# ScalarE's drains moved one row group sooner, into the hold

## The chip, the cores and the metric

One core of one Trainium2 chip. The metric is device time in microseconds (us); a run's "span" is what the profile covers of it, from the first to the last instruction, some 1.3 us less.

## The reference

```python
# x: 16 x 2048 x 256, W: 256 x 256, rank 16, all float32
x_flat = x.reshape(-1, in_dim)
y = x_flat @ W
lora_out = x_flat @ lora_A
lora_out = lora_out * lora_E
lora_out = lora_out @ lora_B
y = y + scale * lora_out
# ... reshaped to batch x seq x out_dim
```

So 33.55 MB go in, 33.55 MB come out, and one 256 x 256 matrix (W plus the low-rank part, folded into it at the start) multiplies it all.

## The kernel before

The rows are cut into 4 chunks of 8.39 MB. Three "homes" in SBUF, the memory on the chip, hold a chunk each; results overwrite their inputs there. A chunk is worked through in 16 row groups, 64 in all, numbered from 0: GpSimd casts a group to bf16, TensorE transposes it, VectorE copies the transposition out of PSUM (the memory that TensorE writes to), TensorE multiplies, ScalarE copies the product from PSUM back into the home. SyncE issues the loads ("L") and stores ("S") in this order, all on one queue; behind the letter stand the chunk, its first row and the row after its last, of 64 in each partition ("A" loads `lora_A`):

```python
ORDER = [
    ("A",),
    ("L", 0, 0, 16),
    ("L", 0, 16, 40),
    ("L", 0, 40, 64),
    ("L", 1, 0, 32),
    ("L", 1, 32, 64),
    ("L", 2, 0, 64),
    ("S", 0, 0, 40),
    ("S", 0, 40, 64),
    ("L", 3, 0, 32),
    ("L", 3, 32, 64),
    ("S", 1, 0, 64),
    ("S", 2, 2, 62),
    ("S", 3, 0, 64),
]

SHARED = 2
END_ROWS = 2
SHARES = (slice(108, 113), slice(0, 108), slice(113, P))

HELD = (2, 0)
HOLDERS = (("S", 0, 0, 40),)

WARM_UP = 2

VECTOR_DRAINS = 12
GPSIMD_DRAINS = 10
SCALAR_DRAINS = 22

CG = 4
GPC = ROWS // CG
N_GROUPS = N_CHUNKS * GPC
```

SyncE's part. A load into a home waits for the stores of the chunk that was there; a store waits for a count that ScalarE raises:

```python
# ... (inside the loop over ORDER)
            kind, c, s, e = op
            at_home = home(c)[:, s:e, :]
            if kind == "L":
                for st in stored:
                    if st[1] == c - N_HOMES and st[2] < e and s < st[3]:
                        sync.wait_ge(stored[st], 16)
                ins = sync.dma_start(out=at_home, in_=x_chunks[c, :, s:e, :]).then_inc(loaded[op], 16)
                if n == 1:
                    opening.append(ins.ins.name)
            else:
                sync.wait_ge(s_done, ends.index((c * ROWS + e - 1) // CG) + 1)
                sync.dma_start(out=y_chunks[c, :, s:e, :], in_=at_home).then_inc(stored.get(op, stored_rest), 16)
        sync.wait_ge(shared_stored, 16 * len(SHARES))
```

VectorE, GpSimd and ScalarE each have a row of drains, which wait for chunk 2's load and then are executed, without working on any data:

```python
    def drain(engine, n):
        for op, landed in loaded.items():
            if op[1:3] == HELD:
                engine.wait_ge(landed, 16)
        for _ in range(n):
            engine.drain()
```

GpSimd is what makes the hold: chunk 2's first group (number 32) waits until chunk 0's first store has landed. At the end it issues small stores of the first two and last two of chunk 2's 64 rows in each partition ("the small stores" below), on a queue of its own.

```python
        for g in range(N_GROUPS):
            c, b = g // GPC, g % GPC * CG
            for op, landed in loaded.items():
                if op[1:3] == (c, b):
                    gpsimd.wait_ge(landed, 16)
            if (c, b) == HELD:
                drain(gpsimd, GPSIMD_DRAINS)
                for op in HOLDERS:
                    gpsimd.wait_ge(stored[op], 16)
            if g >= NS:
                gpsimd.wait_ge(s_turned, g - NS + 1)
            gpsimd.tensor_copy(out=stage[g % NS][:], in_=home(c)[:, b:b + CG, :]).then_inc(s_stage[g % UNROLL], 1)

        gpsimd.wait_ge(s_turned, N_GROUPS - NS + 1)
        gpsimd.drain().then_inc(s_stage[N_GROUPS % UNROLL], 1)
        gpsimd.wait_ge(s_shared, 1)
        for p in SHARES:
            share(gpsimd, p, shared_stored)
```

ScalarE, before:

```python
        for g in range(N_GROUPS):
            c, b = g // GPC, g % GPC * CG
            if (c, b) == HELD:
                drain(scalar, SCALAR_DRAINS)
            scalar.wait_ge(s_y, g + 1)
            scalar.copy(out=home(c)[:, b:b + CG, :], in_=psum_y[g % NY][:]).then_inc(s_free[(g + NY) % UNROLL], 1)
            if (c, b + CG) == (SHARED, ROWS):
                scalar.drain().then_inc(s_shared, 1)
            if g in ends:
                scalar.drain().then_inc(s_done, 1)
```

TensorE runs one group ahead, so that `turn(32)` stands in front of `multiply(31)`; that is why ScalarE's copy of group 31, the last of chunk 1, waits for the hold to end:

```python
        def turn(i, result=None):
            words = stage[i % NS][:].bitcast(FP32)
            staged = s_stage[i % UNROLL]
            for b in range(CG):
                if b == 0:
                    tensor.wait_ge(staged, 1)
                if b == CG - 1 and result is not None:
                    tensor.wait_ge(s_free[result % UNROLL], 1)
                ins = tensor.transpose(psum_xt[i % NT][:, b, :], words[:, b, :], ident[:])
                if b == 0:
                    ins.then_inc(staged, -1)
            ins.then_inc(s_turned, 1)
        # ...
        with tensor.Fori(0, N_GROUPS // UNROLL):
            for i in range(UNROLL):
                turn(i + 1, i)
                multiply(i)
```

## Time and profile before

| | before |
|---|---|
| time, median of the first 3 runs | 161.29 us (161.27 to 161.30) |
| chunk 2 landed; hold ended | 62.70; 75.04 us |
| copy of group 31; copy of group 32 starts | 79.11; 81.45 us |
| chunk 2's, chunk 3's store issued | 101.94; 122.82 us |
| chunk 1's, 2's, 3's store landed | 121.61; 139.97; 159.99 us |

Every time here is counted from the span's start. The page gives the shares over the span. The table by stretch gives them stage by stage. The chain of waits follows the last instruction back through what released it. The list of SyncE's waits says how long SyncE stood at each of its instructions. The prediction shows the lines.

```profile
SPq L300 <- SPq L300: 3.2, 1, 3.2
```

Line 300 is SyncE's very last wait, for the large stores. It began 3.2 us before it was met: everything else, the wait for the small stores and the closing steps of all engines, was over 3.2 us before the end.

### The profile page before, as it was taken

Reading aid. Unit: us, or ns where it says so; the run is one execution under the profiler, and the core shown is the slowest. Engines: PE = TensorE matmul, PEld = TensorE weight load, DVE = VectorE, ACT = ScalarE, POOL = GpSimd, SP = SyncE. Lnnn points to the kernel's source line nnn. Section 1 sums busy time; section 2 is a strip of 40 time slices with the busy share of each in tenths; the row PEclk is TensorE's granted clock in tenths of the full one; section 3 lists DMA queues with packets and bytes.
Section 4 is the critical chain, followed back from the end, with each engine's and each line's share of the span. In section 5 each row is a group of like instructions: output and inputs, shape, how many; then the busy total and the mean of one; then the engine's idle time right before and its main releaser. Section 6 shows DMA issues by size and latency. Waiting matters only on the chain.

```text
span 160.0 us, 2070 instructions
## 1 busy us (share of the span) xinstructions
PE 96.5 (60%) x782; PEld 84.4 (53%) x782; DVE 45.4 (28%) x66; ACT 66.0 (41%) x65; POOL 69.3 (43%) x73
## 2 busy tenths in 40 slices
PE   2769999999999900000999999999994000000000
PEld 1246899999999900000789999999993000000000
DVE  0113355555555500000155555555550000000000
ACT  3001477777777720000257777777775000000000
POOL 1072577777787400002577777778762000000000
PEclk9999999999999995555599999999999555555555
DMA  7999999999969997999999999989979997989986
GB/s 269 427 448 436 412 440 467 451 393 418 631 262 524 475 311 328 403 420 434 412 465 428 401 475 426 532 377 410 524 308 446 480 485 305 544 342 481 441 360 262
DMA packets 2451, 67.43 MB, mean 421 GB/s; under 512 B 512, under 2 KB 528, under 8 KB 784
## 3 DMA queue, kind: packets, MB, share of 16 engines
q1 hardware_dynamic: 2016, 66.60, 97.4%
q0 software_dynamic: 224, 0.52, 0.9%
q10 hardware_dynamic: 208, 0.28, 0.6%
q14 instruction: 3, 0.02, 0.0%
HBM read 33.85 MB, written 33.55 MB: 421 GB/s over the span
## 4 chain that ended last, share of the span: by engine, by line
PE 38%; DMA 33%; ACT 3%; POOL 1%; issue 1%; ACTq 0%; SPq 0%
DMA out_dram<-home 28%; PE psum_y L269 24%; PE psum_xt L258 13%; DMA home<-in_x_dram 5%; ACT home L221 3%; POOL stage L200 1%; PE psum_y L291 1%; SPq L147 0%; ACTq L175 0%; ACTq L225 0%
## 5 line engine op out<-in xcount | busy, mean ns | idle before, releaser
L200 POOL CAST stage<-home 128x1024 bf16<-128x1024 f32 x64 | 66.6, 1042 | 48.6 <-PE psum_xt L258 22.1
L221 ACT COPY home<-psum_y 128x1024 f32<-128x1024 f32 x64 | 64.7, 1012 | 54.8 <-PE psum_y L269 54.8
L269 PE MATMUL psum_y<-weff,xt 128*128 128x256 bf16 x512 | 69.1, 280 | 0.0
L242 DVE COPY xt<-psum_xt 128x1024 bf16<-128x1024 bf16 x64 | 44.3, 692 | 66.2 <-PE psum_xt L258 66.2
L258 PE MATMUL psum_xt<-ident,stage 128*128 128x128 f32 x260 | 42.2, 286 | 22.3 <-POOL stage L200 22.3
L269 PEld LDWEIGHTS psum_y<-weff,xt 128*128 128x128 bf16 x512 | 51.5, 101 | 6.2
L258 PEld LDWEIGHTS psum_xt<-ident,stage 128*128 128x128 f32 x260 | 32.4, 148 | 25.2 <-issue 23.6
L282 PE MATMUL psum_y<-ident 128*128 128x512 f32 x4 | 3.8, 1101 | 2.9 <-POOL ident L180 2.9
L282 PEld LDWEIGHTS psum_y<-ident 128*128 128x128 f32 x4 | 1.2, 325 | 3.9 <-POOL ident L180 2.9
L230 DVE TENSOR_SCALAR ate<-psum_y,e_sb 16x256 f32<-16x256 f32 x1 | 0.5, 471 | 7.2 <-DMA e_sb<-in_lora_E_dram 7.2
L168 POOL DMA_DIRECT2D out_dram<-home x3 | 2.0, 676 | 1.0 <-PE psum_xt L258 1.0
L221 ACT ACT_TABLE_LOAD x1 | 1.3, 1283 | 2.1 <-SPq L304 2.1
L291 PE MATMUL psum_y<-b_sb,ate 16*128 16x256 f32 x4 | 2.1, 670 | 0.0
L291 PEld LDWEIGHTS psum_y<-b_sb,ate 16*128 16x128 f32 x4 | 1.2, 320 | 0.5 <-issue 0.3
L246 DVE TENSOR_TENSOR weff<-w_sb,psum_y 128x512 bf16<-128x512 f32 x1 | 0.7, 689 | 1.4 <-PE psum_y L291 1.4
L285 PEld LDWEIGHTS psum_y<-ident,a_sb 128*16 128x16 f32 x2 | 0.3, 138 | 1.2 <-issue 1.2
L178 POOL MEMSET ident<- 128x128 f32 x1 | 0.2, 205 | 1.7 <-SPq L304 1.7
L285 PE MATMUL psum_y<-ident,a_sb 128*16 128x128 f32 x2 | 0.6, 421 | 0.0
L180 POOL TENSOR_SCALAR_AFFINE_SELECT ident<-ident 128x128 f32<-128x128 f32 x1 | 0.3, 284 | 0.2 <-POOL ident L178 0.2
L326 POOL MEMSET const-float32-0.0<- 128x1 f32 x1 | 0.1, 94 | 0.2 <-issue 0.2
L326 POOL MEMSET const-bfloat16-1.0<- 128x1 bf16 x1 | 0.1, 97 | 0.0
L326 POOL MEMSET const-uint8-127<- 128x1 uint8 x1 | 0.1, 97 | 0.0
(1 smaller groups left out, 0.1 us busy)
## 6 DMA issues: line engine op xcount, KB each, us to landing
home<-in_x_dram SPq DMA_DIRECT2D x4, 4096.0 KB, 24.4
out_dram<-home SPq DMA_DIRECT2D x1, 7680.0 KB, 38.0
home<-in_x_dram SPq DMA_DIRECT2D x2, 3072.0 KB, 16.8
out_dram<-home SPq DMA_DIRECT2D x1, 5120.0 KB, 45.2
out_dram<-home SPq DMA_DIRECT2D x1, 3072.0 KB, 44.6
home<-in_x_dram SPq DMA_DIRECT2D x1, 2048.0 KB, 7.7
out_dram<-home POOLq DMA_DIRECT2D x1, 432.0 KB, 30.2
w_sb<-in_W_dram ACTq DMA_DIRECT2D x1, 256.0 KB, 2.8
```

The lines of the kernel that those rows point to most:

```text
L168: engine.dma_start(out=ends_of(y_chunks[SHARED]), in_=ends_of(home(SHARED))).then_inc(landed, 16)
L200: gpsimd.tensor_copy(out=stage[g % NS][:], in_=home(c)[:, b:b + CG, :]).then_inc(s_stage[g % UNROLL], 1)
L221: scalar.copy(out=home(c)[:, b:b + CG, :], in_=psum_y[g % NY][:]).then_inc(s_free[(g + NY) % UNROLL], 1)
L230: vector.tensor_scalar(out=ate[:], in0=psum_y[0][:R, :KT, :P], scalar1=e_sb[:], scalar2=float(scale), op0=ALU.mult, op1=ALU.mult,).then_in ...
L242: vector.tensor_copy(out=xt[g % NX][:], in_=psum_xt[g % NT][:].bitcast(BF16)).then_inc(s_xt[g % UNROLL], 1)
L246: vector.tensor_add(out=weff[:], in0=w_sb[:], in1=psum_y[1][:, :KT, :]).then_inc(s_free[0], 1)
L258: ins = tensor.transpose(psum_xt[i % NT][:, b, :], words[:, b, :], ident[:])
L269: ins = tensor.matmul(psum_y[i % NY][:, b, :], xt[i % NX][:, b, t::KT], weff[:, t, :], start=(t == 0), stop=(t == KT - 1),)
L282: tensor.matmul(psum_y[1][:, :2, :], ident[:], ident[:, None, :].to_broadcast([P, 4, P]), start=True, stop=True)
L285: ins = tensor.transpose(psum_y[0][:R, t, :P], a_sb[:, t, :], ident[:])
L291: ins = tensor.matmul(psum_y[1][:, t, :], ate[:, t, :], b_sb[:], start=True, stop=True)
L326: nc = _bacc.Bacc("TRN2", target_bir_lowering=False, num_devices=1)
```

## The change

The intent: take ScalarE's drains out from between two copies that have work waiting, and have them executed while ScalarE stands idle in the hold. The count grows from 22 to 26, because the copy of group 31 and its marking drain, which stood in front of the drains, now stand behind; two more are a reserve.

```diff
--- before.py
+++ after.py
@@ -43,7 +43,7 @@
 
 VECTOR_DRAINS = 12
 GPSIMD_DRAINS = 10
-SCALAR_DRAINS = 22
+SCALAR_DRAINS = 26
 
 CG = 4
 GPC = ROWS // CG
@@ -215,7 +215,7 @@
             opening.append(ins.ins.name)
         for g in range(N_GROUPS):
             c, b = g // GPC, g % GPC * CG
-            if (c, b) == HELD:
+            if (c, b + CG) in (HELD, (HELD[0] - 1, HELD[1] + ROWS)):
                 drain(scalar, SCALAR_DRAINS)
             scalar.wait_ge(s_y, g + 1)
             scalar.copy(out=home(c)[:, b:b + CG, :], in_=psum_y[g % NY][:]).then_inc(s_free[(g + NY) % UNROLL], 1)
```

Of the two places that the new condition names, only the second exists: a chunk has no group at row -4, so the drains stand ahead of the copy of group 31 alone.

## The prediction

> **What bounds the kernel now.** I read the page first, for which resource is full; then the table by stretch, for whether it is full in every stage; then the chain of waits around the drains, for what the change can take away; last the queue of the stores, for whether anything taken away there can reach the end.
>
> The page of the kernel before, its DMA rows:
>
> ```profile
> PEclk9999999999999995555599999999999555555555
> DMA  7999999999969997999999999989979997989986
> ...
> q1 hardware_dynamic: 2016, 66.60, 97.4%
> ...
> q14 instruction: 3, 0.02, 0.0%
> ...
> HBM read 33.85 MB, written 33.55 MB: 421 GB/s over the span
> ```
>
> The 16 DMA engines are full from the second slice to the last. No compute engine is above 60% over the span. The three packets of the instruction queue matter below. The table by stretch, one row for each stage from the hold to the end:
>
> ```profile
> core 0: us, PE busy (x) PEld busy (x) DVE busy (x) ACT busy (x) POOL busy (x), PEclk, DMA share, GB/s
> 63.00:75.00 12.00, 0.00 (x0) 0.00 (x0) 0.00 (x0) 0.00 (x0) 0.00 (x0) 0.50 1.00 433
> 75.00:82.40 7.40, 6.12 (x39) 5.24 (x39) 2.08 (x3) 1.96 (x3) 5.16 (x5) 0.67 0.99 425
> 82.40:101.90 19.50, 19.45 (x179) 18.04 (x178) 10.36 (x15) 15.15 (x16) 15.24 (x15) 1.00 1.06 454
> 101.90:122.80 20.90, 19.81 (x182) 18.17 (x180) 9.70 (x15) 16.19 (x16) 14.93 (x16) 1.00 1.02 439
> 122.80:140.00 17.20, 0.00 (x0) 0.00 (x0) 0.00 (x0) 0.00 (x0) 0.00 (x0) 0.54 1.00 429
> ```
>
> The DMA share is 0.99 or more in each (over 1.00 because packets straddle the edges of a stretch), at some 430 GB/s whether the engines compute or stand idle. Compute stands still for the 12 us of the hold and is over for good at 122.8 us, 37 us ahead of the end. So compute has room; the transfers have none.
>
> The chain of waits around the drains (start us, us, what):
>
> ```profile
> 77.37 1.72 PE psum_y L269 x8
> 79.09 0.02 issue
> 79.11 1.01 ACT home L221
> 80.12 0.04 ACTq L225
> ...
> 80.89 0.03 issue
> 80.92 0.35 issue
> 81.27 0.14 ACTq L175
> 81.42 0.04 issue
> 81.45 1.02 ACT home L221
> 82.48 0.04 issue
> 82.52 0.33 PE psum_xt L258
> ```
>
> ScalarE's last copy of chunk 1 (79.11) runs after the hold, because the multiplication that it copies stands on TensorE behind the transposition of chunk 2's first row group, which the hold keeps back. Only then come the drains, so they stand between two copies with work waiting. This chain calls itself the one that ended last, but it covers only what the queue of issues can be traced through; it ends at 122.8 with the last issue. The issues, over the stretch from 101 us on:
>
> ```profile
> out_dram<-home SPq DMA_DIRECT2D x1, 7680.0 KB, 38.0
> ...
> out_dram<-home SPq DMA_DIRECT2D x1, 37.2
> ```
>
> These are the stores of chunks 2 and 3. The first is issued at 101.94, so it lands at 139.97; the second is issued at 122.82 and lands at 159.99, and the span ends at 160.0. Both lie on the same queue. Chunk 3's store holds 8.39 MB; landing 20.02 us after the one in front of it, it moved at 419 GB/s. It therefore waited in a full queue for some 17.1 us (139.97 less 122.82) before its turn. That is the slack of all compute.
>
> **What the Trainium skill says.** "DMA: Bandwidth & Descriptors", section "Where 436 GB/s comes from": 435.2 GB/s is the ceiling of the 16 SBUF ports, while the side of HBM would bind at about 358. The trace agrees with the first only: 433 GB/s during the hold. So the transfers are at their ceiling. Section "Queues, rings and completion order" of that page: each DMA engine takes the queues by turns, packet by packet, and one row belongs to the runtime, instruction refill among its uses. The trace agrees that refills share the engines: queue 14 moved 8192-byte packets of 0.31 us each. "Runtime: NRT & Kernel Launch", section "Instruction fetch mechanics": an engine's instructions are refilled block by block by its own sequencer while it runs on, "mostly hidden". The trace shows 8192-byte packets, two of them at 67.83 and 67.84 us (VectorE's and GpSimd's drains ended at 63.2 and 63.4), and one at 84.82, 3.55 us after the odd drain at 81.27. I read these as the refills of the three engines; who asked for each is inferred from the order in time. "Perfetto Trace Analysis", section "Sequencer-only Instruction (DRAIN, etc)": a drain's record holds its execution alone, not fetch and decode. The trace agrees: 8 ns recorded, at a pitch of 33 ns.
>
> **The change part by part.**
>
> *Removed: the drains between two copies.* 20 pitches of 33.6 ns (80.23 to 80.91), then 0.35 us of issue and a last drain of 0.14 us; with ends the gap from the copy's end (80.12) to the next copy's start (81.45) is 1.33 us. Its multiplication ended at 80.83 (last matmul at 80.56, 0.27 us), and a copy starts 0.02 us after one, so without drains the copy starts at 80.85. Gain on ScalarE: 0.60 us. The marking drain after the last row group of a chunk stays; elsewhere (28.79, then 30.10) it doesn't stretch the 1.31 us from copy to copy.
>
> *What of that reaches TensorE.* It waits for ScalarE once: the transposition at 82.52, whose predecessor started at 82.20, against a pitch of 0.109 us. It lost 82.52 - 82.31 = 0.21 us. That copy would now end at 81.86, before 82.31, so the wait goes. From there on to 122.8 us TensorE has one row group per 1.31 us with no other wait on ScalarE, so everything shifts by 0.21 us: the last issue from 122.82 to about 122.61.
>
> *Added: 26 drains in front of the copy of row group 31.* They wait for chunk 2's load, which landed at 62.70 (VectorE's drains started at 62.73). 26 at 33.6 ns make 0.87 us, with the same odd step of 0.49 us some 1.4 us: done at about 64.1, 11 us before the hold ends at 75.04. Cost on any path: none.
>
> *Why 26 and not 22.* I count the odd drain as the 22nd in the row. In front of it in program order stood one copy and one marking drain that now stand behind, and waits with a copy may be instructions of their own. 24 drains would reach the same instruction count; 26 leave two over. So the step from one block to the next should stay inside the drains, and the refill move from 84.8 us to near the other two at 67.8.
>
> *DMA.* No byte is added: three refills before, three after. One packet of 0.31 us changes its place on one of 16 engines that have no idle time in either place; that engine's sum is the same.
>
> *Sum.* 0.60 us off ScalarE, 0.21 us off TensorE, and the last store is issued 0.21 us sooner into a queue with 17.1 us still to move: 0.00 us at the end. By the same reasoning chunk 2's store, issued at 101.94 or 101.73, stands behind chunk 1's, whose last landing is at 121.61.
>
> **The rivals.**
>
> *The compute gain reaches the end in full.* Then 161.29 - 0.21 = 161.08. For it: the chain does run through these drains. Against: the 17.1 us above. I give it one in twenty.
>
> *The refill hurts where it goes.* Three refills together in the hold could fall on one DMA engine. If that is the last to land chunk 0's first store, the hold ends up to 0.31 us later and the compute after it is 0.31 - 0.21 = 0.1 us later. Loads waiting on that store would be issued later too, but the queue then still holds chunk 0's second store, which took from 75.04 to 82.37. So again 0; if an engine did run dry, 0.3 us: 161.6.
>
> *Moved transfers share the path differently.* GpSimd's three small stores of the shared end rows are issued 0.2 us sooner (119.05 to 118.84) on their own queue, and the engines' ends lie 0.9 us apart (159.08 to 159.99). A packet of the large stores is 65536 bytes and takes 2.42 us, so a reordering at such a boundary can move the last engine by a few tenths, either way. This is what I expect to make up any difference that is seen.
>
> *A missed block edge.* If the step falls on the copy after the drains, ScalarE loses 0.5 us there again and TensorE keeps its 0.21 us wait: 161.29.
>
> **Range and chances.** The rivals reach from 161.08 less two tenths to 161.6, and the three runs before lie within 0.03 us of each other. I take 161.25 us: zero from the main path, with a slight lean to the first rival. Eight times in ten between 160.95 and 161.60. 2% is 3.2 us; nothing in the change has that size, since the whole gap on ScalarE is 1.33 us. Faster by over 2%: 0.01; within 2%: 0.98; slower by over 2%: 0.01.
>
> **What would show it.** Right: ScalarE's drains recorded between 62.7 and about 64.2; copy 32 starting some 1.3 to 1.7 us after copy 31 instead of 2.34; TensorE's 0.3 us wait for ScalarE gone from the list of waits; the refill near 68 us; the last store issued near 122.6 and still landing near 160.0. Wrong: a last landing that moves by as much as the last issue, or a DMA row with a gap near the hold. The prediction as a whole fails if the total rate changes by a per cent or more, which none of these steps gives a reason for.

## The result and the profile after

| | runs | median | ratio to before | 95% interval |
|---|---|---|---|---|
| before, beside it | 6 | 161.28 us (160.90 to 161.38) | | |
| after | 6 | 161.12 us (160.89 to 161.28) | 0.9994 | 0.9981 to 1.0007 |

A ratio is the mean time of one kernel's runs over that of the other's in the same rounds, so not quite the ratio of the medians. The time is the same, and inside the predicted range.

The page of the kernel after, its DMA rows:

```profile
DMA  7999999999979997989999999998998997989976
...
q1 hardware_dynamic: 2016, 66.60, 97.4%
...
HBM read 33.85 MB, written 33.55 MB: 422 GB/s over the span
```

The queue is as full as before. What changed is ScalarE; its timeline after (start us, us, engine, line, operation, count, idle before and releaser):

```profile
79.07 1.01 ACT L221 COPY home<-psum_y 128x1024 f32<-128x1024 f32 x1 [21.87 <-PE psum_y L269]
80.75 1.01 ACT L221 COPY home<-psum_y 128x1024 f32<-128x1024 f32 x1 [0.67 <-PE psum_y L269]
82.06 1.01 ACT L221 COPY home<-psum_y 128x1024 f32<-128x1024 f32 x1 [0.30 <-PE psum_y L269]
```

Copy 32 follows copy 31 by 1.68 us instead of 2.34. Where the 26 drains went, from the instructions of their line:

```profile
L175 ACTq DRAIN  x26: 8/8/143, 62.3 to 63.6; - x26
```

All are over 11 us before the hold ends at 75.00. The chain of waits after has no ScalarE and no issue between two pieces of TensorE:

```profile
77.33 1.71 PE psum_y L269 x8
79.03 0.81 PE psum_xt L258 x4
79.84 0.87 PE psum_y L269 x8
80.72 0.44 PE psum_xt L258 x4
81.15 0.87 PE psum_y L269 x8
82.03 0.44 PE psum_xt L258 x4
```

The last store is issued at 122.44, 0.39 us sooner, and is still 37.3 us from landing (the issues from 101 us on):

```profile
out_dram<-home SPq DMA_DIRECT2D x1, 7680.0 KB, 38.2
...
out_dram<-home SPq DMA_DIRECT2D x1, 37.3
```

So both large stores stand in the queue 0.1 to 0.2 us longer than before (37.2 and 38.0 there).

The last landing, 159.72 us, is 0.27 us sooner than before, which taken alone comes near the prediction's sign of being wrong. But this trace was ahead before the change could act: chunk 2's load landed at 62.25 us instead of 62.70, and the first of the moved drains ran at 62.27. By the packet records, the packets begun before 62 us had exceeded the median time of their size by 6.4 us less in all than in the kernel before, which is 0.40 us for each of the 16 DMA engines. So this one pair of profiles doesn't show that the last issue moved the end; the repeated runs below decide.

### The profile page after: what moved, and what is told of

It reads as the page before. It is cut to its first block, busy times and chain, and to the rows that moved or that the text cites. A ratio compares the mean times of both kernels' runs of the same rounds, so it can differ in the third digit from the quotient of the medians. Undisturbed runs are those within 1.5% of the kernel's fastest.

```text
span 159.8 us, 2074 instructions
## 1 busy us (share of the span) xinstructions
PE 96.1 (60%) x782; PEld 84.2 (53%) x782; DVE 45.4 (28%) x66; ACT 66.1 (41%) x65; POOL 69.3 (43%) x73
## 4 chain that ended last, share of the span: by engine, by line
PE 40%; DMA 33%; POOL 1%; ACT 1%; issue 0%; SPq 0%; ACTq 0%
DMA out_dram<-home 28%; PE psum_y L269 25%; PE psum_xt L258 14%; DMA home<-in_x_dram 5%; POOL stage L200 1%; ACT home L221 1%; PE psum_y L291 1%; SPq L147 0%; ACTq L225 0%
```

## The experiments

The theory: the end is set by the transfer queue, which is full; compute has slack, and a stall of ScalarE under that slack is lost in it. Rival 1: ScalarE's stall reaches the end. Rival 2: what counts is where the refill of ScalarE's instructions falls. Each kernel was timed beside the kernel before on one chip.

### The count alone, in the old place

```diff
-SCALAR_DRAINS = 22
+SCALAR_DRAINS = 26
```

> The kernel before with ScalarE's count alone changed, 22 to 26, in the old place. Theory (the transfer queue sets the end, compute has some 17 us of slack): copy 32 starts 4 x 0.0335 = 0.13 us later than in the kernel before, the last issue moves from 122.8 to about 122.95, the time stays 161.1 to 161.3 us, ratio 1.000 within 0.001. Rival 1 (ScalarE's stall reaches the end in full): 0.13 us longer than before, ratio 1.0008. Rival 2 (the place of the instruction refill decides): as before, since the refill stays near 85 us.

Measured: 161.22 us, before 161.24; ratio 0.9997 (0.9984 to 1.0011). ScalarE's timeline:

```profile
79.32 1.01 ACT L221 COPY home<-psum_y 128x1024 f32<-128x1024 f32 x1 [23.59 <-PE psum_y L269]
81.88 1.01 ACT L221 COPY home<-psum_y 128x1024 f32<-128x1024 f32 x1 [1.55 <-PE psum_y L269]
```

Between the copies stand 2.56 us, 0.22 more than before. The last issue came at 123.95, a whole us later than expected: in this profiled run TensorE's full clock was granted only from 82.52 us, against 79.86 before. Yet the store landed at 160.03, 0.04 us after that of before. The last issue 1.13 us later, the end the same. But SyncE's last wait, 3.2 us before, is down to this:

```profile
SPq L300 <- SPq L300: 1.0, 1, 1.0
```

The small stores were issued 1.13 us later too (120.18 for 119.05) and landed 2.25 us later (157.41 for 155.16).

### The place alone, with the old count

```diff
-SCALAR_DRAINS = 26
+SCALAR_DRAINS = 22
```

(against the changed kernel, as all that follow)

> The changed kernel with the old count, 22. By the count of instructions the odd one, at which ScalarE steps to its next block, is the 64th recorded; with 22 drains it falls on the marking drain behind the copy of row group 31, so after the hold, and the refill moves back from 67.6 to about 82 or 83 us. That drain waits for a copy of 1.01 us anyway, so the step of 0.36 us should be hidden and copy 32 should start 1.68 us after copy 31, as in the changed kernel. Theory: 161.1 to 161.3 us. Rival 1: as the changed kernel, 0.2 us under before. Rival 2 (place of the refill): as the kernel before, not the changed one, if the difference between the two is real at all.

Measured: 161.21 us, before 161.24; ratio 0.9996 (0.9983 to 1.0010). The time is as the theory has it, but the refill is not where I put it. All three refills left at 67.72 to 67.82 us, as with 26 drains, although the 64th record, the marking drain, ran only at 79.26. So the refill did not wait for that instruction, and my count of drains needed (24) was too high: 22 suffice to have the refill in the hold. Copy 32 started 1.83 us after copy 31, with TensorE as releaser, whose full clock came at 80.14 us here.

### None of ScalarE's drains

```diff
-SCALAR_DRAINS = 26
+SCALAR_DRAINS = 0
```

> The changed kernel with none of ScalarE's drains (the others' stay). The block step then falls on the copy of row group 53, near 108 us, in the middle of compute, and the refill near 110 to 113 us. [...] no stall should show: TensorE's wait for ScalarE stays away, last issue near 122.5. Theory: 161.1 to 161.3 us, same as all others: moving the drains and deleting them are worth the same, nothing at the end. Rival 2 (the refill's place decides): a time that differs from the changed kernel's by more than the spread.

Measured: 160.96 us, before 161.24; ratio 0.9983 (0.9970 to 0.9997). The refill now lay at 107.68 us, and ScalarE's timeline around it shows no stall, one copy per 1.31 us:

```profile
105.52 1.01 ACT L221 COPY home<-psum_y 128x1024 f32<-128x1024 f32 x1 [0.30 <-PE psum_y L269]
106.83 1.01 ACT L221 COPY home<-psum_y 128x1024 f32<-128x1024 f32 x1 [0.30 <-PE psum_y L269]
108.14 1.01 ACT L221 COPY home<-psum_y 128x1024 f32<-128x1024 f32 x1 [0.30 <-PE psum_y L269]
```

The interval just leaves out 1.

### The changed kernel again

> The changed kernel again, to see if its 0.16 us lower median stands. Theory: ratio within 0.001 of 1 and an interval that includes it. Rival 1: TensorE's 0.21 us reach the end: ratio 0.9987 with an interval that excludes 1.

Measured: 161.23 us, before 161.24; ratio 1.0004 (0.9991 to 1.0018). The 0.16 us between the first medians did not come back. Rival 1's ratio of 0.9987 lies outside; the first runs' interval (0.9981 to 1.0007) still held it.

### No drains, again

> The changed kernel without ScalarE's drains again, since its interval (0.9970 to 0.9997) just left out 1. Theory: chance among many intervals; ratio within 0.0012 of 1 this time and including it. If deleting the drains is worth something that moving them is not: 0.998 again.

Measured: 161.15 us, before 161.09; ratio 0.9997 (0.9983 to 1.0012). So the first was most likely chance, as one in twenty such intervals is. Deleting the drains and moving them come to the same: nothing. Rival 2 falls with it: the refill at 84.8, 67.6 or 107.7 us makes no difference that these runs can see.

### A stall twenty times as large

```diff
             if g in ends:
                 scalar.drain().then_inc(s_done, 1)
+            if (c, b + CG) == (HELD[0] - 1, HELD[1] + ROWS):
+                for _ in range(18):
+                    scalar.copy(out=w_sb[:], in_=home(c)[:, b:b + KT, :])
+                    scalar.drain()
```

Copies into one buffer without a drain count as a race.

> The changed kernel with 18 idle copies of 128x512 on ScalarE (into a buffer no longer used), each with a drain, between the copies of row groups 31 and 32: a stall of an estimated 12 to 13 us, some twenty times the 0.60 us that the change takes away, in the same place. Theory: TensorE stops for nearly all of it, the last issue moves from 122.4 to about 134, still ahead of the landing of chunk 2's store at 139.7, so the end does not move: 161.0 to 161.5 us. Rival 1 (a stall there reaches the end): 173 us.

Measured: 164.11 us, before 161.25; ratio 1.0173 (1.0156 to 1.0190). The theory as I had it missed: a stall of 12.3 us (18 copies at 0.68 us) should have cost nothing and cost 2.9 us. It did not cost 12 either, as rival 1 has it. The last issue came at 136.26, 3.7 us before 139.97, when chunk 2's store landed in the kernel before (here it landed at 141.28), and the queue shows no gap. SyncE's waits in this kernel:

```profile
SPq L161 <- ACTq L225: 83.8, 4, 31.5
...
SPq L147 <- DMA out_dram<-home: 24.2, 1, 24.2
SPq L155 <- DMA out_dram<-home: 7.4, 1, 7.4
SPq L344 <- PEq L344: 0.9, 2, 0.8
```

The last wait, of 3.2 us in the kernel before, is gone from the list. What stands there is the wait for the small stores (line 147, 24.2 us). They landed at 160.82, against 154.90 in the changed kernel. From there SyncE and the other engines need 1.66 us of closing steps (160.84 to 162.50); in the changed kernel the same steps ran from 154.92 on, hidden beneath the last large store. The large stores landed at 161.20, 1.48 us later than in the changed kernel, and the rest of the closing steps lies behind that, 1.28 us more than there. Together 2.76 us, which is the difference of the spans (162.51 less 159.75).

So there is a second path to the end, of which the prediction says nothing: GpSimd's small stores. Why they take long also shows. They landed 9.5 to 34.8 us after their issue in the changed kernel for 0.5 MB. The trace fits packets that take turns with those of the large stores: 224 packets are 14 on each of 16 engines if they are spread evenly, so 13 large packets of 2.42 us lie between the first and the last, an estimate of 31.4 us from these figures; in the changed kernel the first small packet started at 123.20 and the last at 154.55, 31.35 us apart. The fit is no rule: in the run with 18 idle copies they are 23.2 us apart, and 88 of the 128 packets that carry data went out between 138 and 140 us, where chunk 2's store ended. But issued from 132.49 on instead of 118.66, the last landed only 0.4 us ahead of the large stores instead of 4.8.

### The same, twice as long

36 copies in place of 18.

> The same with 36 idle copies, an estimated 24 to 26 us. Theory: now beyond the slack of 17.3 us (139.72 less 122.44): the last issue near 147, the queue runs empty, and the end is that issue plus some 20 us for the last store and 1 to 2 us until its first bytes move: span 168 to 170, time 169 to 171 us. Rival 1: 185 us. If compute could not reach the end at all: 161.2 us.

Measured: 170.66 us, before 161.25; ratio 1.0590 (1.0546 to 1.0634), a time as expected. The table by stretch:

```profile
101.00:122.00 21.00, 16.07 (x123) 14.28 (x124) 6.92 (x10) 14.89 (x18) 10.41 (x10) 0.75 0.82 356
122.00:128.00 6.00, 6.00 (x58) 5.58 (x56) 3.46 (x5) 4.69 (x5) 4.83 (x5) 1.00 0.00 0
128.00:148.50 20.50, 19.79 (x182) 18.16 (x180) 9.68 (x14) 15.85 (x16) 14.89 (x16) 1.00 0.95 398
```

The columns are the stretch, its length, busy us (and count) of PE, PEld, DVE, ACT and POOL, the granted clock, the DMA share and GB/s. From 122 to 128 the DMA share is 0.00: the queue has run dry, since chunk 1's store landed at 121.33 and chunk 2's was issued only at 128.02. Chunk 3's followed at 148.90 and landed 20.7 us later, at 169.63. Beyond the slack, compute does set the end. The slack that gave way is that of chunk 2's store, 19.9 us (121.41 less 101.55 in the changed kernel), not the 17.3 us of the last store from which I reckoned: it was issued 26.5 us later.

This run also tests why the small stores take long. Here their packets fell between the two large stores (the first started at 147.13, chunk 3's first packet at 149.73), and they landed 3.1 to 3.8 us after their issue, where beside large packets they took up to 34.8.

### The bytes

```diff
             else:
                 sync.wait_ge(s_done, ends.index((c * ROWS + e - 1) // CG) + 1)
+                if c == N_CHUNKS - 1:
+                    e -= CG
+                    at_home = home(c)[:, s:e, :]
```

> The changed kernel, but the last store leaves out 4 of its 64 rows in each partition (wrong result on purpose: these rows are never written; compute and every issue as they were). 0.524 MB less at 430 GB/s is 1.22 us. Theory: the whole of it comes off the end, 159.9 us within 0.2, ratio 0.9925. Rival 1 (the chain of compute sets the end): no change.

Measured: 160.10 us, before 161.25; ratio 0.9929 (0.9912 to 0.9945). 1.15 us of the expected 1.22 came off. Leaving out 0.8% of the bytes does to the time what moving the drains cannot. For the theory it shows less than I expected of it: these bytes move after the last issue, so the end would come sooner as well if compute set the moment of that issue. The two are told apart by the runs that move the issue (the next two).

### No hold

```diff
             if (c, b) == HELD:
                 drain(gpsimd, GPSIMD_DRAINS)
-                for op in HOLDERS:
-                    gpsimd.wait_ge(stored[op], 16)
```

> The changed kernel without the hold: GpSimd starts chunk 2 once it has landed (62.3 us) and no longer waits for chunk 0's first store (75.0). Compute after it runs up to 12.7 us sooner, the last issue near 110 us instead of 122.4. Theory: the transfers keep their order and their rate, so 161.1 us within 0.4. Rival 1: up to 12 us shorter. A third possibility, that the hold was there for something else (transfers that are slower beside compute, or a lower TensorE clock), would show as a longer time with a lower rate of transfers between 63 and 75 us.

Measured: 161.48 us, before 161.25; ratio 1.0017 (1.0000 to 1.0033). Copy 31 ran at 67.14, 11.9 us sooner, chunk 2's store was issued at 97.25, 4.3 us sooner, and the last at 118.50, 3.9 us sooner. I had expected about 110. Compute gave the rest back in a wait for chunk 3's first load, which keeps its time because the queue does: it landed at 92.03, GpSimd's casts stood from 85.5 to 92.1 us, and TensorE came back with half its clock until 96.68. The last landing: 159.93. Even 12 us taken from compute in this place make nothing. Nor does the third possibility show; the stretch of the hold, now with all engines at work (columns as above):

```profile
63.00:75.00 12.00, 10.70 (x76) 9.37 (x77) 4.15 (x6) 5.21 (x6) 8.23 (x8) 0.73 1.02 438
```

The transfers moved at 438 GB/s beside compute and at 430 in the idle hold of the changed kernel.

### The stall late, past the small stores

```diff
             if g in ends:
                 scalar.drain().then_inc(s_done, 1)
+            if g == N_GROUPS - 2:
+                for _ in range(18):
+                    scalar.copy(out=w_sb[:], in_=home(SHARED)[:, CG:CG + KT, :])
+                    scalar.drain()
```

> The same stall as in the run with 18 idle copies (12.3 us), but between ScalarE's copies of row groups 62 and 63, so that it holds back chunk 3's store alone and not GpSimd's small stores of the shared rows. New theory for the 2.9 us of that run: the small stores have their own path with far less slack than the 17 us; they landed at 160.82, and what follows their landing (1.66 us up to the wait for the large stores) was no longer hidden. If so, the late stall costs nothing: last issue near 134.7, small stores landing near 154.9 as in the changed kernel, 161.2 us within 0.4. Rival (any 12 us stall of compute costs some 3 us, by issuing the last store nearer to its turn): 164 us.

Measured: 161.37 us, before 161.09; ratio 1.0021 (0.9999 to 1.0044). SyncE's waits:

```profile
SPq L147 <- DMA out_dram<-home: 19.2, 1, 19.2
SPq L155 <- DMA out_dram<-home: 7.0, 1, 7.0
SPq L304 <- SPq L304: 3.5, 1, 3.5
```

The last issue came at 135.42, about as late as with the early stall (136.26), and this time the small stores landed at 154.92 and the last wait is back, 3.5 us. The last store landed 24.6 us after its issue, at 160.05, instead of 37.3 us:

```profile
out_dram<-home SPq DMA_DIRECT2D x1, 24.6
```

The 13 us came out of its time in the queue. So a late last store alone costs little or nothing; the early stall's cost came by another way. The rival's 164 us is out.

### Without the small stores, without and with the stall

```diff
-    ("S", 2, 2, 62),
+    ("S", 2, 0, 64),
...
-        sync.wait_ge(shared_stored, 16 * len(SHARES))
...
-        for p in SHARES:
-            share(gpsimd, p, shared_stored)
```

> Control for the next run: the changed kernel without the small stores, chunk 2 stored whole by one issue, without the wait for them. Same bytes. How even the 16 engines end without the small stores is not known: 161 to 163 us; the small stores were presumably put in because this is longer.

> The control above with the stall of 12.3 us between the copies of row groups 31 and 32, which cost 2.9 us with the small stores in place. New theory: without them nothing is left that the stall can reach: within 0.4 us of the control. Rival: some 3 us over the control.

Measured, both beside before at 161.09 us: without the stall 161.82 us, ratio 1.0044 (1.0025 to 1.0062); with it 162.57 us, ratio 1.0092 (1.0073 to 1.0110). The stall costs 0.75 us here, more than the 0.4 that I allowed and far less than 2.9. So most of its cost needs the small stores, as the new theory has it, and a remainder doesn't. The last landing moved by 0.61 us (160.47 to 161.08), all of it already there when chunk 2's store landed (141.16 to 141.77). That store was issued at 115.71, still 4.2 us before the first part of chunk 1's landed; no gap in the queue shows. The 0.6 us are those of a single part: of the 16 parts in which the last store landed, 15 were there by 159.72 without small stores and with the stall, and by 159.87 without the stall; the sixteenth came at 161.08 and 160.47. Why that one stays behind is open.

The 1.48 us by which the large stores landed later in the run with 18 idle copies are not explained by the small stores, as one might think from the difference. By the packet records, that run's packets took 15.7 us more in all than the changed kernel's, about 1 us on each engine, and nearly all of it before 101 us, ahead of the small stores; 6.7 of the 15.7 lay before the stall began (80.41), so the stall didn't cause them. What shows as the small stores' part is the 1.28 us of closing steps, and perhaps the 0.4 us by which that run's time exceeds its span by more than in the others, which no profile covers; the rest of the 2.9 us stays open.

## Why the prediction was right, point by point

- **The bound.** Right. The queue sets the end: without the hold (last issue 3.9 us sooner) and with a last issue 13 us later the time stayed within some 0.3 us (ratios 1.0017 and 1.0021), and compute set the end where the queue ran dry (1.0590), apart from the path of the small stores (below). That fewer bytes shortened the time by nearly their share fits, but doesn't decide it.
- **ScalarE's drains.** Right. They ran from 62.3 to 63.6; 64.1 had been foreseen for a load that landed 0.45 us later than it did.
- **The gain on ScalarE.** Right in size: 0.66 us less from copy 31 to copy 32, 0.60 foreseen.
- **TensorE.** The wait for ScalarE is gone from the list of waits. The last issue moved by 0.39 us and not by 0.21. The stall was worth 0.27 us, since the first matmul behind it had also started 0.06 us late (82.52 to 82.69, at a pitch of 0.109). The other 0.12 us are not the change's doing: the hold ended 0.04 us sooner, and the full clock was granted from 79.67 instead of 79.86 us, which took 0.07 us off by the transposition of group 34 (80.55 against 80.67). The run with 26 drains in the old place shows the clock's effect the other way, and larger. The granted clock moves compute by more than the change does (about 1.0 us there), and it too is lost in the slack.
- **The sum of 0.00 us.** Right, by the repeat: 1.0004 (0.9991 to 1.0018). The 0.16 us of the first median did not come back, and the profiled pair's earlier landing goes with a head start from before the drains. The lean of 0.04 us to the first rival had no ground.
- **"That is the slack of all compute."** Wrong. The 17.1 us hold for chunk 3's store alone. The small stores had 3.2 us, and a stall of 12.3 us broke through there. The change's 0.39 us lie far below both, so the prediction came out right, but to that extent by luck: it hadn't looked at this path, where its slack was five times too wide.
- **The refill and the count of 26.** The place is right (67.54 to 67.63 us). The reason is not: with 22 drains the refill lay there as well. What the odd drain of 0.14 us is, with 0.36 us ahead of it, stays open; it is the 64th record of ScalarE before and after.
- **The rivals.** A gain in full (0.9987): outside the repeat's interval, and against it stand the runs that move the last issue by more without moving the end. The refill that hurts: no sign, at three different places. Moved transfers: no difference was left to explain.

## What to carry to other kernels

Before you take a stall away from an engine, look for how long the transfers issued after it wait for their turn: here 17 us for the last store, so that 0.6 us on ScalarE were worth nothing. Do this for every transfer that the end waits for, the small ones too: the list of the issuing engine's last waits gives the margin of each in one line (3.2 us here). Such a margin is in time of landing and not of issue: an issue 1.13 us later took 2.2 us of these 3.2. A stall made larger on purpose, in the same place, measures such a slack; here it showed a path that reading had missed.

## What the Trainium skill lacked or had wrong

- "DMA: Bandwidth & Descriptors", section "Where 436 GB/s comes from": it has HBM bind transfers between HBM and SBUF at about 358 GB/s, and leaves out the condition that the same page's section "Bandwidth" gives, that both cores of an HBM domain are streaming. Here, with the kernel on one core, such transfers ran at 430 to 433 GB/s for 12 us of the hold, and at 421 over the whole span; only its port ceiling of 435.2 fits.
- "Runtime: NRT & Kernel Launch", section "Instruction fetch mechanics": it has refills in blocks of 16 KiB. Here the instruction queue moved three packets of 8192 bytes in the span, at times that fit one for each of three engines; that these are whole refills is inferred. It does not say either whether a refill stalls an engine: with the one at 107.68 us in the midst of copies, these kept their 1.31 us. (The step of 0.36 us among the drains stays unexplained.)
- "Perfetto Trace Analysis", section "Sequencer-only Instruction (DRAIN, etc)": it gives no figure for what a drain takes of the sequencer. Here ScalarE's followed each other every 33.6 ns with 8 ns recorded, so 22 cost some 0.74 us, not 0.18.
- "DMA: Bandwidth & Descriptors", section "Queues, rings and completion order": it states the turns, packet by packet, but not what follows for a small store beside a large one: 0.5 MB in 224 packets took up to 34.8 us to land beside packets of 2.42 us. Nor that this can serve a purpose: with the small stores the last store's 16 parts landed within 0.9 us of each other (158.82 to 159.72), without them within 1.96 us (158.51 to 160.47), for 0.7 us of time (161.82 against 161.09 of the kernel before).
